# Second MLP product with 512-column matmuls over all eight PSUM banks, and a third late buffer for weights

## The chip, the cores and the metric

The kernel runs on one core of one Trainium2 chip. Its time is the device time of one launch in microseconds (us); less is better. The core has five engines that run side by side and each take their instructions strictly in the order written: TensorE (PE, matrix products), VectorE (DVE), ScalarE (ACT), GpSimd (POOL) and SyncE (SP, which here only issues transfers). Transfers from memory, whoever issues them, are carried by 16 DMA engines that all queues share. Matrix products write to PSUM, a small memory of eight banks, each with 512 single-precision columns on 128 partitions.

## The reference

One decoder layer over 512 tokens with 1024 features. Only its end matters here, the squared-ReLU MLP and the final norm:

```python
def rms_norm(x, g):
    xf = x.astype(jnp.float32)
    y = xf * lax.rsqrt(jnp.mean(xf * xf, axis=-1, keepdims=True) + NORM_EPS)
    return (y * g.astype(jnp.float32)).astype(x.dtype)
...
        x = x + cross_attention(h, mem_n, w_xq[l], w_xk[l], w_xv[l], w_xo[l])
        h = rms_norm(x, norm_mlp[l])
        x = x + jnp.square(jax.nn.relu(h @ w_ff1[l])) @ w_ff2[l]
    return rms_norm(x, norm_final)
```

`w_ff1` is 1024 x 4096 and `w_ff2` is 4096 x 1024. Before the MLP come a combined projection, two kinds of mixing heads, an output projection and a cross-attention; the change does not touch them.

## The kernel before

**Split operands.** Every large product works on numbers split in two: `hi`, rounded by ACT to the matrix unit's reduced format, and `lo`, the rest, which DVE subtracts. A product then takes three matmuls for each pair of 128 x 128 weights and its activations: upper weights with upper activations, upper weights with lower activations, lower weights with upper activations. Weights arrive in units of 128 x 1024, that is eight blocks. The function `split_raw` turns a unit that has landed in a raw buffer into `wh` (ACT, 1024 columns) and `wl` (DVE, 1024 columns).

**The two MLP products.** Each is a 2 x 2 block product done in the seven-product way (Strassen in Winograd's form), so it needs sums of weight blocks and sums of activation blocks. Tokens are cut into two halves of 256, so a matmul there has 256 columns.

The *first* product runs `f1_group(j)` for j = 0 to 7. A group has seven steps, one for each product, of 2 x 4 x 3 = 24 matmuls. Its weights come as transfers named A, B, C, c and D (`f1_load`, L277). B and c get a second block added on the way by a GpSimd transfer; D and the later meaning of A are made by DVE sums (`f1_add`). `f1_prep(j, s)` (L288) is called two steps ahead of the matmuls that use its unit (`SPLIT_AHEAD`); it emits the split of one unit and, at fixed s, the loads of the group after: B at s = 1, C at 3, A at 4, c at 5, D at 6. B, C and c rotate over three raw buffers (`RAWS`), A and D over two buffers of the late pool (`raw_tile`, L227). The results of the steps are taken out of PSUM by `evac` inside `f1_group`, on ACT and DVE; some of that work is put off into a list, `rest`, which the next step runs.

The *second* product (`PLAN`, L1287, and the loop below it) runs seven products p of eight weight units each: units 0 to 3 are the first half of the contraction for the four output tiles n, units 4 to 7 the second half. A unit has 8 x 3 = 24 matmuls of 256 columns, a product 192, the whole 1344. The accumulators X, Y and Z are pairs of banks; a bank holds two output tiles of 256 columns. X is used by products 0, 2, 4 and 6, which go on adding to what it holds, Y by 1 and 3, Z by 5. After each pair of output tiles DVE adds the bank (128 x 2 x 256) into the residual `x1`; from product 3 on, ACT and DVE also do their share of the final norm (`norm_part`). For each product ACT and DVE also split four activation tiles (`make_op`, tiles `op`, 128 x 2048: upper half and lower half side by side), and DVE makes the sums of activation blocks (`make_sum`, tiles `g`), four each for products 2, 3 and 4.

**What sets the order.** From `f1_group` on, the order on each engine is the order in which the program emits instructions (`manual_schedule`). In the second product a unit begins with `need`, which emits the loads as far ahead as buffers allow (at most `RAWS + 2` = 5 raw units open) and the split of the unit two ahead; then `f1_rest`, `need_op` and `need_sum`, then the matmuls, then the evacuation. `wl` rotates over three buffers, so the DVE split of the unit two ahead waits until PE has finished the unit before.

In PSUM eight banks are two pools of four, `pacc` (X, Z) and `pside` (Y and small things). In SBUF the late pool lies where the early pool (`ep`) was. Some weight sums for the second product (tiles `u`) are made in DRAM by transfers of SP and of POOL during the first product (`more_sums`).

Nearly all instructions pass through the helper at L115, so the profile shows that line for them; they are told apart by the names of their tiles.

Of the kernel before, what the change touches and what calls it, by code (L numbers as in the profile page):

```python
# [8 lines left out]
F32 = mybir.dt.float32  # L9
# [6 lines left out]
P = 128  # L16
D = 1024
T = 512
M = 256
# [12 lines left out]
MLP = 8 + 8 + 4 + 8 + 4 + 4 + 4 + 4 + 8 + 8 + 8  # L32
FF2 = MLP + 7 * 8
# [89 lines left out]
def hybrid_layer(ctx: ExitStack, tc: tile.TileContext, xT, memT, ws, vecs, consts, rots, out):  # L123
    nc = tc.nc
    pace = Pace()
    V, A, PE = (pace.engine(e, t) for e, t in ((nc.vector, "dve"), (nc.scalar, "act"), (nc.tensor, "pe")))
    SY, PO = pace.engine(nc.sync, "dma"), pace.engine(nc.gpsimd, "pool")
    cpool = ctx.enter_context(tc.tile_pool(name="cpool", bufs=1))
# [2 lines left out]
    dram = ctx.enter_context(tc.tile_pool(name="dram", bufs=1, space=bass.MemoryType.DRAM))  # L131
    early = ExitStack()
    ep = early.enter_context(tc.tile_pool(name="early", bufs=1, reuse_waits="tile"))
    pacc = ctx.enter_context(tc.tile_pool(name="pacc", bufs=4, space=bass.MemoryType.PSUM))
    pside = ctx.enter_context(tc.tile_pool(name="pside", bufs=4, space=bass.MemoryType.PSUM))
    ordered = tc.manual_schedule()
    ordered.__enter__()
    WBUFS, N8, N2, N2E, N8L = 4, 12, 14, 8, 3
# [21 lines left out]
    def acc_bank(name):  # L160
        return pacc.tile([P, T], F32, tag="acc", name=name)

    def side_bank(name):
        return pside.tile([P, T], F32, tag="ps", name=name)
# [5 lines left out]
    raws, his, los, late, n8 = {}, {}, {}, [], [1]  # L170
    state = {"load": 0, "split": 0}
    LOAD_AHEAD, SPLIT_AHEAD, RAWS = 6, 2, 3
# [13 lines left out]
    def two(ap):  # L186
        return ap.rearrange("p (n c) -> p n c", n=2)
# [11 lines left out]
    def add(dst, src):  # L199
        return nc.gpsimd.dma_start(dst, src, accum_op=ALU.add, max_dma_last_dim=4 * D)  # L200
# [25 lines left out]

    def raw_tile(name, in_late):  # L227
        if in_late:
            return late[0].tile([P, D], F32, tag="rawl", name=name, bufs=2)
        return wpool.tile([P, D], F32, tag="raw", name=name, bufs=RAWS)  # L230

    def load_unit(parts=((0, D),)):
        u = state["load"]
        raws[u] = raw_tile(f"wr{u}", u >= FF2 and (u - FF2) % 5 in (1, 3))
        for a, b in parts:
            SY.dma_start(raws[u][:, a:b], sources[u][:, a:b])
        state["load"] += 1
        if SUMS_FROM <= u < MLP:
            more_sums()
# [37 lines left out]
    def f1_load(j, what):  # L277

        r, c = {"A": (0, 0), "B": (0, 0), "C": (1, 1), "D": (1, 0)}[what.upper()]
        t = f1raw[what, j] = raw_tile(f"w{what}{j}", what in "AD")  # L280
        nc.sync.dma_start(two(t), E[r][c][j].rearrange("n p c -> p n c"))
        if what in "Bc":
            nc.gpsimd.dma_start(two(t), E[0][1][j].rearrange("n p c -> p n c"), accum_op=ALU.add)
# [4 lines left out]
    def f1_prep(j, s):  # L288

        split_raw(split_begin(), f1raw[("ABCAcDd" if j == 7 else "ABDCAcD")[s], j], 0, D)  # L290
        if s == 1:
            f1_add(j, "A", "B", "C")
        if j == 7:
            if s == 1:
                f1_load(j, "d")
                state["load"] = FF2
            elif s > 2:
                load_unit()
            if s == 3:
                f1_add(j, "d", "d", "A")  # L300
        elif s == 1:
            f1_load(j + 1, "B")
        elif s == 3:
            f1_add(j, "D", "D", "A")
            f1_load(j + 1, "C")
        elif s == 4:
            f1_load(j + 1, "A")
        elif s == 5:
            f1_load(j + 1, "c")
        elif s == 6:  # L310
            f1_load(j + 1, "D")
        if s in (2, 6):
            more_sums()

    def need(u):
        marks.append(last_mm[0])
        if MLP <= u + SPLIT_AHEAD < FF2:
            f1_prep(*divmod(u + SPLIT_AHEAD - MLP, 7))
            return
        last = MLP if u < MLP else UNITS  # L320
        most = RAWS if u < MLP else RAWS + 2
        want_load, want_split = min(last, u + LOAD_AHEAD + 1), min(last, u + SPLIT_AHEAD + 1)
        while state["split"] < want_split or state["load"] < want_load:
            if state["load"] < want_load and state["load"] - state["split"] < most:
                load_unit()
            elif state["split"] < want_split:
                split_unit()
            else:
                break
        if MLP - 6 <= u < MLP - 2:  # L330
            for what in ("A", "B", "CD", "c")[u - MLP + 6]:
                f1_load(0, what)
# [53 lines left out]
    def mm(o, l, r, start, stop):  # L386
        last_mm[0] = PE.matmul(o, l, r, start=start, stop=stop, skip_group_check=True)
        since[0] += 1
        if since[0] >= GAP:
            pump()  # L390
# [223 lines left out]
    u = 4  # L614
# [242 lines left out]
        yield from norm_rows(S, M, rbm, rcm)  # L857

    mem = {}
    rbm = cpool.tile([P, M], F32, name="rbm")  # L860
    rcm = cpool.tile([P, 2], F32, name="rcm")
    fm_stage(u, x_act, T, ev_g, "hg", ONE * 4)
    u += 4
# [325 lines left out]
    def need_sum(i):  # L1189
        while sum_state[0] < min(28, i + 1):  # L1190
            make_sum(*divmod(sum_state[0], 4))
            sum_state[0] += 1
# [3 lines left out]
    def make_op():  # L1196

        i = op_state[0]
        op_state[0] += 1
        need_sum(i)  # L1200
        src = OPS[i // 4](i % 4)
        both = l8(F32R, f"op{i}").rearrange("p a b -> p (a b)")
        hi, lo = (x.rearrange("p (k c) -> p k c", k=4) for x in (both[:, :D], both[:, D:]))
        if i // 4 == 2:
            A.activation(hi, src, AF.Copy, scale=-1.0)
            V.scalar_tensor_tensor(lo, src, -1.0, hi.bitcast(F32), op0=ALU.mult, op1=ALU.subtract)
        else:
            A.activation(hi, src, AF.Copy)
            V.tensor_sub(lo, src, hi.bitcast(F32))
        ops[i] = [(hi[:, k], lo[:, k]) for k in range(4)]  # L1210

    def need_op(i):
        while op_state[0] < min(28, i + 1):
# [5 lines left out]
        f1_group(j)  # L1219
        u += 7  # L1220

    X, Z = ([acc_bank(f"{x}{b}") for b in range(2)] for x in "XZ")
    Y = [side_bank(f"Y{b}") for b in range(2)]

    def place(h, t, b):

        return x1[h][:, 2 * b:2 * b + 2, t * half:(t + 1) * half]

    def into(h, t, op):
        def evac(banks, n):  # L1230
            if n % 2:
                d = place(h, t, n // 2)
                getattr(V, op)(d, d, two(banks[n // 2]))
        return evac

    rbf = rb2
# [19 lines left out]

    def final_half(nb, S, q):

        ps = side_bank("fs")
        yield [S[:, :half]]  # L1260
        smm(ps[:, :half], ones, S[:, :half], True, False)
        yield [q[:, :half]]
        smm(ps[:, :half], ones, q[:, :half], False, True)
        r = rbf[:, nb * half:(nb + 1) * half]
        rsqrt_of(r, ps[:, :half], D)
        for eng, a, b in ((V, 0, 2), (V, 2, 4), (V, 4, 7), (V, 7, 8)):
            x = xg(nb, a, b)
            eng.tensor_mul(x, x, r[:, None, :].to_broadcast([P, b - a, half]))
            SY.dma_start(out[nb, :, a:b], x)

    def ends(h, t, op):
        add = into(h, t, op)

        def evac(banks, n):
            add(banks, n)
            if n % 2:
                norm_part(h, t, n - 1)
                norm_part(h, t, n)
        return evac

    def ends_last(banks, n):
        d = x1[0][:, n, half:]
        V.tensor_add(d, d, two(banks[n // 2])[:, n % 2])
        norm_part(0, 1, n)


    PLAN = ((X, True, into(0, 0, "tensor_add")), (Y, True, into(1, 1, "tensor_sub")),  # L1287
            (X, False, into(1, 0, "tensor_sub")), (Y, False, ends(1, 0, "tensor_sub")),
            (X, False, ends(1, 1, "tensor_sub")), (Z, True, ends(0, 0, "tensor_add")), (X, False, ends_last))

    for p, (banks, begins, after) in enumerate(PLAN):
        for j in range(8):
            i, c, n = 8 * p + j, j // 4, j % 4
            if i >= 52:
                n = LAST[n]
            need(FF2 + i)
            f1_rest()
            need_op(4 * p + 2 * c + 1 + (0, 1, 2, 2)[j % 4])
            need_sum(4 * p + 2 * c + (3, 3, 3, 4)[j % 4])
            hi, lo = his[FF2 + i], los[FF2 + i]  # L1300
            acc = two(banks[n // 2])[:, n % 2]
            for k in range(8):
                a_hi, a_lo = ops[4 * p + 2 * c + k // 4][k % 4]
                w_hi, w_lo = hi[:, k * P:(k + 1) * P], lo[:, k * P:(k + 1) * P]
                mm(acc, w_hi, a_hi, begins and c == 0 and k == 0 and n % 2 == 0, False)
                mm(acc, w_hi, a_lo, False, False)
                mm(acc, w_lo, a_hi, False, c == 1 and k == 7)
            if c:
                after(banks, n)
    drain(("fin", 0))  # L1310
    drain(("fin", 1))
    ordered.__exit__(None, None, None)
# [74 lines left out]
```

## Time and profile before

| | |
|---|---|
| runs | 758.73, 760.60, 762.17 us; median 760.60 us |
| profiled execution | 756.95 us, of it 755.2 us span (first to last instruction) |
| PE busy | 735.1 us, 97% of the span, 4696 matmuls |
| DVE busy | 545.5 us, 72% |
| ACT busy | 415.5 us, 55% |
| mean granted TensorE clock | 0.996 of full speed |
| first MLP product | matmuls start from 413.06 us to 582.79 us |
| second MLP product | from 582.91 us; the last matmul is over at 746.03 us |
| after it | final norm of the last half and stores, to 755.2 us |

A group of the profile names the tile written, the tiles read, the shape, how many instructions and their mean duration. The durations of matmuls overlap, since they are pipelined: a matmul of 256 columns is shown as 283 ns long, while the next one starts 120 ns after it. What a matmul costs in a full stretch is therefore read from the distance between starts, or from a row of the chain of waits, which gives a stretch's length and the number of matmuls in it. The chain of waits follows the execution back from its last instruction to whatever released each step.

### The profile page before, as it was taken

What the parts mean: (1) busy time and instruction counts of PE and PEld (TensorE: products, weight loads), DVE (VectorE), ACT (ScalarE), POOL (GpSimd) and SP (SyncE); (2) the same over time, 40 slices, a digit from 0 to 9 for tenths busy, and PEclk for the clock granted to TensorE, in tenths of its full rate; (3) what the DMA queues carried; (4) which work ended last, traced back from release to release, by engine and by line L of the source; (5) the groups of instructions that cost most, each with busy time, mean ns of one, the idle gap of its engine ahead of it and who ended that gap; (6) DMA issues with size and microseconds to landing.
All of it is one profiled execution on the core that took longest, in us unless ns stands there. A gap on an engine that the chain in (4) does not pass through costs nothing.

```text
span 755.2 us, 11996 instructions
## 1 busy us (share of the span) xinstructions
PE 735.1 (97%) x4696; PEld 664.0 (88%) x4696; DVE 545.5 (72%) x891; ACT 415.5 (55%) x634; POOL 49.4 (7%) x62
## 2 busy tenths in 40 slices
PE   7999999999999999999999999998999999999995
PEld 5888888777787998888888999998899999999995
DVE  6898554887766656767377878786778778877783
ACT  6773447345855454545365655465446655546562
POOL 1000000000111200011000111221110000000000
PEclk9999999999999999999999999999999999999999
DMA  7425334544689996479726688898975655545641
GB/s 274 149 76 167 112 116 135 167 135 132 183 207 238 207 313 258 118 160 278 254 77 147 169 249 221 187 208 215 212 213 169 204 189 193 173 162 168 207 156 57
DMA packets 44441, 137.03 MB, mean 181 GB/s; under 512 B 4544, under 2 KB 6976, under 8 KB 43744
## 3 DMA queue, kind: packets, MB, share of 16 engines
q1 hardware_dynamic: 34944, 110.64, 42.8%
q0 software_dynamic: 8960, 25.17, 19.1%
q8 instruction: 37, 0.61, 0.3%
q10 hardware_dynamic: 480, 0.45, 0.2%
q14 instruction: 20, 0.16, 0.1%
HBM read 134.15 MB, written 35.65 MB: 225 GB/s over the span
## 4 chain that ended last, share of the span: by engine, by line
PE 87%; DMA 4%; ACT 3%; DVE 3%; issue 2%; SPq 0%; DVEq 0%; ACTq 0%
PE X L115 19%; PE Y L115 12%; PE xo L115 7%; PE mkq L115 6%; PE xq L115 6%; PE wo L115 5%; DMA wA<-in_ws_dram 3%; PE hf L115 3%; PE Z L115 3%; PE hg L115 3%; PE mv L115 3%; PE memv L115 3%; PE hq L115 3%; PE hi L115 3%; PE memk L115 2%
## 5 line engine op out<-in xcount | busy, mean ns | idle before, releaser
L115 ACT ACTIVATE wh<-wr 128x1024 fp32r<-128x1024 f32 (+2 forms) x126 | 130.4, 1041 | 121.2 <-PE wo L115 19.6
L115 DVE TENSOR_TENSOR wl<-wr,wh 128x1024 fp32r<-128x1024 f32 (+2 forms) x126 | 151.5, 1205 | 40.7 <-ACT wh L115 26.4
L115 PE MATMUL X<-op,wh 128*128 128x256 f32 x512 | 92.7, 283 | 0.0
L115 PEld LDWEIGHTS X<-op,wh 128*128 128x128 f32 x512 | 79.9, 192 | 0.1
L115 PE MATMUL X<-op,wl 128*128 128x256 f32 x256 | 72.7, 284 | 0.6 <-DVE wl L115 0.6
L200 POOL DMA_DIRECT2D u<-in_ws_dram x32 | 31.0, 968 | 328.5 <-PE hg L115 201.1
L115 PEld LDWEIGHTS X<-op,wl 128*128 128x128 f32 x256 | 49.1, 192 | 0.8 <-DVE wl L115 0.8
L115 PE MATMUL Y<-OS,wh 128*128 128x256 f32 x256 | 47.2, 284 | 0.2 <-ACT t L115 0.2
L115 PE MATMUL X<-OS,wh 128*128 128x256 f32 x256 | 46.5, 283 | 0.0
L115 PE MATMUL Y<-op,wh 128*128 128x256 f32 x256 | 46.2, 283 | 0.0
L115 PEld LDWEIGHTS Y<-OS,wh 128*128 128x128 f32 x256 | 39.9, 192 | 0.5 <-ACT t L115 0.4
L115 PEld LDWEIGHTS Y<-op,wh 128*128 128x128 f32 x256 | 39.9, 192 | 0.0
L115 PEld LDWEIGHTS X<-OS,wh 128*128 128x128 f32 x256 | 39.9, 192 | 0.0
L115 PE MATMUL Y<-op,wl 128*128 128x256 f32 x128 | 36.2, 283 | 0.0
L115 PE MATMUL X<-OS,wl 128*128 128x256 f32 x128 | 36.2, 283 | 0.0
L115 PE MATMUL Y<-OS,wl 128*128 128x256 f32 x128 | 36.2, 283 | 0.0
L115 ACT ACTIVATE g<-t 128x512 f32<-128x512 f32 x32 | 19.0, 624 | 29.2 <-DVE t L115 29.2
L115 ACT ACTIVATE op<-g 128x1024 fp32r<-128x1024 f32 x28 | 29.2, 1045 | 0.5 <-PE X L115 0.5
L115 DVE TENSOR_TENSOR op<-g,op 128x1024 fp32r<-128x1024 f32 x24 | 29.3, 1219 | 0.0
L115 ACT ACT_TABLE_LOAD x22 | 28.2, 1283 | 1.5 <-PEq L1375 1.2
L115 PE MATMUL mkq<-xhi,wh 128*128 128x512 f32 x64 | 26.7, 417 | 0.0
L115 ACT ACTIVATE t<-X 128x256 f32<-128x256 f32 x32 | 11.3, 375 | 27.8 <-PE X L115 27.7
(312 smaller groups left out, 2114.2 us busy)
## 6 DMA issues: line engine op xcount, KB each, us to landing
wr<-in_ws_dram SPq DMA_DIRECT2D x90, 512.0 KB, 4.3
u<-in_ws_dram POOLq DMA_DIRECT2D x32, 512.0 KB, 7.7
wr<-u SPq DMA_DIRECT2D x32, 512.0 KB, 3.4
u<-in_ws_dram SPq DMA_DIRECT2D x16, 512.0 KB, 3.9
u<-u SPq DMA_DIRECT2D x16, 512.0 KB, 4.7
wA<-in_ws_dram SPq DMA_DIRECT2D x8, 512.0 KB, 6.5
wD<-in_ws_dram SPq DMA_DIRECT2D x8, 512.0 KB, 6.3
wB<-in_ws_dram SPq DMA_DIRECT2D x8, 512.0 KB, 4.3
```

Of the source, the lines that this page charges most:

```text
L115: return f(*args, **kw)
L200: return nc.gpsimd.dma_start(dst, src, accum_op=ALU.add, max_dma_last_dim=4 * D)
```

## The change

- In the second product, the matmul of upper weights with upper activations and that of upper weights with lower activations become one: the moving operand is the pair of 256-column pieces (upper, lower), the result 512 columns, a whole bank. The matmul of lower weights with upper activations adds into that bank's first half. Each output tile now has its own bank, so each accumulator has four banks; X and Y take all eight, and Z's product uses Y again. The two first PSUM pools are closed for this and one of its own is opened.
- Taking a result out means adding both halves of a bank, so `into` and `ends_last` do two DVE additions where there was one. For products 0 to 5 they are put off to the next unit by way of `rest`.
- Sums of activation blocks are emitted two operands earlier (`need_sum`).
- The late pool's raw tag gets three buffers instead of two; in the first product the load of A moves from s = 4 to s = 2; in the second, raw tiles alternate between the pools and up to six may be open instead of five. The tile `rbm` moves to the early pool.

```diff
-    pacc = ctx.enter_context(tc.tile_pool(name="pacc", bufs=4, space=bass.MemoryType.PSUM))
-    pside = ctx.enter_context(tc.tile_pool(name="pside", bufs=4, space=bass.MemoryType.PSUM))
+    banks1 = ExitStack()
+    pacc, pside = (banks1.enter_context(tc.tile_pool(name=n, bufs=4, space=bass.MemoryType.PSUM)) for n in ("pacc", "pside"))
...
-            return late[0].tile([P, D], F32, tag="rawl", name=name, bufs=2)
+            return late[0].tile([P, D], F32, tag="rawl", name=name, bufs=RAWS)
...
-        raws[u] = raw_tile(f"wr{u}", u >= FF2 and (u - FF2) % 5 in (1, 3))
+        raws[u] = raw_tile(f"wr{u}", u >= FF2 and (u - FF2) % 2 == 1)
...
+        elif s == 2:
+            f1_load(j + 1, "A")
         elif s == 3:
             f1_add(j, "D", "D", "A")
             f1_load(j + 1, "C")
-        elif s == 4:
-            f1_load(j + 1, "A")
...
-        most = RAWS if u < MLP else RAWS + 2
+        most = RAWS if u < MLP else 2 * RAWS
...
-        ops[i] = [(hi[:, k], lo[:, k]) for k in range(4)]
+        ops[i] = [both.rearrange("p (x k c) -> p x k c", x=2, k=4)[:, :, k] for k in range(4)]
...
+    banks1.close()
+    pm = ctx.enter_context(tc.tile_pool(name="pm", bufs=1, space=bass.MemoryType.PSUM, reuse_waits="tile"))
+
+    def banks4(name):
+        return [pm.tile([P, 2, T], F32, tag=f"{name}{b}", name=f"{name}{b}", bufs=1) for b in range(2)]
 
     def into(h, t, op):
-        def evac(banks, n):
+        def evac(acc, n):
             if n % 2:
-                d = place(h, t, n // 2)
-                getattr(V, op)(d, d, two(banks[n // 2]))
+                d = x1[h][:, n - 1:n + 1, t * half:(t + 1) * half]
+                for x in range(2):
+                    getattr(V, op)(d, d, acc[n // 2][:, :, x * half:(x + 1) * half])
         return evac
...
-    def ends_last(banks, n):
+    def ends_last(acc, n):
         d = x1[0][:, n, half:]
-        V.tensor_add(d, d, two(banks[n // 2])[:, n % 2])
+        for x in range(2):
+            V.tensor_add(d, d, acc[n // 2][:, n % 2, x * half:(x + 1) * half])
         norm_part(0, 1, n)
...
+    accs = {name: banks4(name) for name in "YX"}
+    for p, (name, begins, after) in enumerate(PLAN):
+        if p == 5:
+            accs[name] = banks4(name)
+        acc = accs[name]
...
-            need_sum(4 * p + 2 * c + (3, 3, 3, 4)[j % 4])
+            need_sum(4 * p + 2 * c + (5, 5, 5, 6)[j % 4])
             hi, lo = his[FF2 + i], los[FF2 + i]
-            acc = two(banks[n // 2])[:, n % 2]
             for k in range(8):
-                a_hi, a_lo = ops[4 * p + 2 * c + k // 4][k % 4]
+                a = ops[4 * p + 2 * c + k // 4][k % 4]
                 w_hi, w_lo = hi[:, k * P:(k + 1) * P], lo[:, k * P:(k + 1) * P]
-                mm(acc, w_hi, a_hi, begins and c == 0 and k == 0 and n % 2 == 0, False)
-                mm(acc, w_hi, a_lo, False, False)
-                mm(acc, w_lo, a_hi, False, c == 1 and k == 7)
-            if c:
-                after(banks, n)
+                mm(two(acc[n // 2][:, n % 2]), w_hi, a, begins and c == 0 and k == 0, False)
+                mm(acc[n // 2][:, n % 2, :half], w_lo, a[:, 0], False, c == 1 and k == 7)
+            if c and p < 6:
+                rest.append(lambda after=after, acc=acc, n=n: after(acc, n))
+            elif c:
+                after(acc, n)
```

What moves on PE, at the start of the second product (X is the accumulator, `op` the split activations, `wh` and `wl` the two parts of the unit's weights). Before:

```order
L115 MATMUL X_5808<-op_5634,wh_5738 128x256 x2
L115 MATMUL X_5808<-op_5634,wl_5739 128x256
L115 MATMUL X_5808<-op_5634,wh_5738 128x256 x2
L115 MATMUL X_5808<-op_5634,wl_5739 128x256
L115 MATMUL X_5808<-op_5634,wh_5738 128x256 x2
L115 MATMUL X_5808<-op_5634,wl_5739 128x256
```

After:

```order
L115 MATMUL X_5817<-op_5634,wh_5738 128x512
L115 MATMUL X_5817<-op_5634,wl_5739 128x256
L115 MATMUL X_5817<-op_5634,wh_5738 128x512
L115 MATMUL X_5817<-op_5634,wl_5739 128x256
L115 MATMUL X_5817<-op_5634,wh_5738 128x512
L115 MATMUL X_5817<-op_5634,wl_5739 128x256
```

Three matmuls of 256 columns have become one of 512 and one of 256; the number of columns is the same, the number of matmuls falls from 1344 to 896.

What moves on SP, in the first product, at the loads for groups 5 and 6 (the names are the transfers A to D). Before:

```order
L281 DMA wB_4796<-in_ws_dram 128x2x512
L281 DMA wC_4872<-in_ws_dram 128x2x512
L281 DMA wA_4908<-in_ws_dram 128x2x512
L281 DMA wc_4945<-in_ws_dram 128x2x512
L281 DMA wD_4976<-in_ws_dram 128x2x512
L281 DMA wB_5042<-in_ws_dram 128x2x512
```

After:

```order
L281 DMA wB_4796<-in_ws_dram 128x2x512
L281 DMA wA_4835<-in_ws_dram 128x2x512
L281 DMA wC_4874<-in_ws_dram 128x2x512
L281 DMA wc_4945<-in_ws_dram 128x2x512
L281 DMA wD_4976<-in_ws_dram 128x2x512
L281 DMA wB_5042<-in_ws_dram 128x2x512
```

The load of A now stands right behind that of B, ahead of C, and before c and D as before.

What moves on DVE, in product 2 of the second MLP product, around the first half of the results (x is the residual, X the accumulator). Before:

```order
L115 TENSOR_TENSOR wl_6492<-wr_6361,wh_6491 128x1024
L115 TENSOR_TENSOR op_6495<-g_3834,op_6495 128x1024
L115 TENSOR_TENSOR x_1899<-x_1899,X_5808 128x2x256
L115 TENSOR_TENSOR wl_6526<-wr_6394,wh_6525 128x1024
L115 TENSOR_TENSOR op_6529<-g_3835,op_6529 128x1024
```

After:

```order
L115 TENSOR_TENSOR wl_6333<-wr_6234,wh_6332 128x1024
L115 TENSOR_TENSOR op_6336<-g_3834,op_6336 128x1024
L115 TENSOR_TENSOR wl_6358<-wr_6259,wh_6357 128x1024
L115 TENSOR_TENSOR x_1899<-x_1899,X_5817 128x2x256 x2
L115 TENSOR_TENSOR op_6363<-g_3835,op_6363 128x1024
```

The addition out of PSUM has become two, and they stand behind the next weight split instead of ahead of it.

More of the change, by code (lines that the diff above doesn't have):

```diff
@@ L859, in hybrid_layer @@
     mem = {}
-    rbm = cpool.tile([P, M], F32, name="rbm")
+    rbm = ep.tile([P, M], F32, name="rbm")
     rcm = cpool.tile([P, 2], F32, name="rcm")
@@ L1220, in hybrid_layer @@
         u += 7
[L1222 to L1227, printed above, removed]
+    banks1.close()
+    pm = ctx.enter_context(tc.tile_pool(name="pm", bufs=1, space=bass.MemoryType.PSUM, reuse_waits="tile"))
+    def banks4(name):
+        return [pm.tile([P, 2, T], F32, tag=f"{name}{b}", name=f"{name}{b}", bufs=1) for b in range(2)]
     def into(h, t, op):
-        def evac(banks, n):
+        def evac(acc, n):
             if n % 2:
-                d = place(h, t, n // 2)
-                getattr(V, op)(d, d, two(banks[n // 2]))
+                d = x1[h][:, n - 1:n + 1, t * half:(t + 1) * half]
+                for x in range(2):
+                    getattr(V, op)(d, d, acc[n // 2][:, :, x * half:(x + 1) * half])
         return evac
@@ L1257, in final_half @@
     def final_half(nb, S, q):
-        ps = side_bank("fs")
+        ps = banks4("Y")[0][:, 0]
         yield [S[:, :half]]
@@ L1272, in ends, with evac @@
         add = into(h, t, op)
-        def evac(banks, n):
-            add(banks, n)
+        def evac(acc, n):
+            add(acc, n)
             if n % 2:
@@ L1279, in ends @@
         return evac
-    def ends_last(banks, n):
+    def ends_last(acc, n):
         d = x1[0][:, n, half:]
-        V.tensor_add(d, d, two(banks[n // 2])[:, n % 2])
+        for x in range(2):
+            V.tensor_add(d, d, acc[n // 2][:, n % 2, x * half:(x + 1) * half])
         norm_part(0, 1, n)
[L1287 to L1291, printed above, removed]
+    PLAN = (("X", True, into(0, 0, "tensor_add")), ("Y", True, into(1, 1, "tensor_sub")),
+            ("X", False, into(1, 0, "tensor_sub")), ("Y", False, ends(1, 0, "tensor_sub")),
+            ("X", False, ends(1, 1, "tensor_sub")), ("Y", True, ends(0, 0, "tensor_add")), ("X", False, ends_last))
+    accs = {name: banks4(name) for name in "YX"}
[3 more added lines that the diff above has]
+        acc = accs[name]
         for j in range(8):
```

## The prediction

> **What bounds the kernel now.** I read the page first: the span, then the busy shares.
>
> ```profile
> span 755.2 us, 11996 instructions
> PE 735.1 (97%) x4696; PEld 664.0 (88%) x4696; DVE 545.5 (72%) x891; ACT 415.5 (55%) x634; POOL 49.4 (7%) x62
> ```
>
> PE is busy almost throughout, so time goes down in two ways only: the same products in fewer PE nanoseconds, or fewer holes. For the price of a matmul I read the chain of waits in order of time, where a row is a stretch, its length in us and its number of matmuls. Stages of 512 columns, then one product of the second MLP product:
>
> ```profile
> 128.37 10.47 PE mkq L115 x46
> 182.20 3.24 PE hg L115 x14
> 278.15 15.88 PE xq L115 x70
> 364.59 48.63 PE xo L115 x214
> ...
> 629.16 23.04 PE X L115 x192
> ```
>
> The last row gives 23.04 / 192 = 0.1200 us for each matmul of 256 columns. Those of 512 cost 48.63 / 214 = 0.2272 (xo), 15.88 / 70 = 0.2269 (xq), 0.2276 (mkq), 0.2314 (hg). So 256 more columns cost 0.1072 us, and a matmul of 256 costs 0.0128 us beyond its columns: a price for each matmul, whatever its length. The three matmuls of a weight block pay it three times.
>
> For the holes I read the waits of PE from 400 to 585 us (total, times, longest), then the chain there:
>
> ```profile
> PE X L115 <- DVE t L115: 4.7, 3, 2.7
> PE Y L115 <- ACT t L115: 0.2, 1, 0.2
> ```
>
> ```profile
> 484.00 7.33 DMA wA<-in_ws_dram
> ...
> 505.24 9.27 DMA wA<-in_ws_dram
> ...
> 528.40 8.34 DMA wA<-in_ws_dram
> ```
>
> PE is named as waiting for a DVE evacuation (t), but the chain leads back to the load of A, three groups running. ACT, DVE and PE of the second case, in order of time:
>
> ```profile
> 514.58 1.06 ACT L115 ACTIVATE wh<-wA 128x1024 fp32r<-128x1024 f32 x1 [3.95 <-DMA wA<-in_ws_dram]
> 515.55 1.04 ACT L115 ACTIVATE wh<-wB 128x1024 fp32r<-128x1024 f32 x1
> ```
>
> ```profile
> 515.67 1.23 DVE L115 TENSOR_TENSOR wl<-wA,wh 128x1024 fp32r<-128x1024 f32 x1 [3.56 <-ACT wh L115]
> 516.82 0.41 DVE L115 TENSOR_TENSOR t<-t,X 128x256 f32<-128x256 f32 x1
> ```
>
> ```profile
> 514.25 0.28 PE L115 MATMUL X<-OBh,wl 128*128 128x256 f32 x1
> 517.28 0.39 PE L115 MATMUL X<-OBh,wh 128*128 128x256 f32 x1 [2.75 <-DVE t L115]
> ```
>
> ACT stood 3.95 us until A landed; DVE stood behind ACT; the evacuation of X, which needs nothing of A, stood behind that split in DVE's queue; and PE could not reuse X.
>
> **The change part by part.**
>
> *A's load (third buffer, s = 4 to s = 2).* SP's issues for one group:
>
> ```profile
> 496.40 0.37 SPq L281 DMA_DIRECT2D wB<-in_ws_dram  x1
> 502.97 0.37 SPq L281 DMA_DIRECT2D wC<-in_ws_dram  x1
> 505.24 0.37 SPq L281 DMA_DIRECT2D wA<-in_ws_dram  x1
> ```
>
> With two buffers A had to wait until the old A was split. With three it takes the buffer of a D that was used up a group earlier, stands right behind B in SP's queue, and can go at about 496.8 instead of 505.24: 8.4 us earlier, against ACT's wait of 3.95. What the holes cost: the two rows above are 3.03 us apart, where 0.12 is normal, so 2.91. The others:
>
> ```profile
> 493.66 0.28 PE L115 MATMUL X<-OBh,wl 128*128 128x256 f32 x1
> 494.11 0.39 PE L115 MATMUL X<-OBh,wh 128*128 128x256 f32 x1 [0.17 <-DVE t L115]
> ...
> 537.42 0.28 PE L115 MATMUL X<-OBh,wl 128*128 128x256 f32 x1
> 539.52 0.39 PE L115 MATMUL X<-OBh,wh 128*128 128x256 f32 x1 [1.82 <-DVE t L115]
> ...
> 543.63 0.41 PE L115 MATMUL X<-OA,wh 128*128 128x256 f32 x2
> ```
>
> They give 0.45 - 0.12 = 0.33 and 2.10 - 0.12 = 1.98. From 539.52 to 543.63 there are 21 matmuls in 4.11 us, where 21 x 0.12 = 2.52 were due: 1.59 more. The clock granted shows why:
>
> ```profile
> 540.00:550.00 10.00, 10.00 (x74) 10.00 (x73) 8.41 (x11) 6.52 (x12) 1.26 (x2) 0.83 0.80 168
> ```
>
> Clock 0.83 (the third number from the end) over ten us is half clock for 3.4 us; so the hole brought a slow stretch with it, which goes too. Sum 2.91 + 0.33 + 1.98 + 1.59 = **6.8 us**. The Trainium skill (TensorE: Matmul & The Clock Gate, HAM oscillation) has the clock fall only after idle gaps of more than about 3.4 us, while here 1.82 us did it and 2.75 us did not; by the rule alone the slow stretch would have another cause and could stay, and the term would be 5.2.
>
> What may be late next is B, whose second block POOL adds:
>
> ```profile
> 501.51 1.23 POOL L283 DMA_DIRECT2D wB<-in_ws_dram  x1 [3.59 <-DMA wB<-in_ws_dram]
> ```
>
> and among the DMA issues the time from issue to landing, 7.0 us in the median:
>
> ```profile
> wB<-in_ws_dram POOLq DMA_DIRECT2D x8, 512.0 KB, 7.0
> ```
>
> So it lands near 501.51 + 7.0 = 508.5. Without the wait for A, ACT comes to B at 514.58 - 3.95 + 1.0 = 511.6. Three us of slack, about what one more 512 KB transfer ahead of it takes. C, c and D are issued as before and no longer share the engines with A. Bounds: 6.8 at most; 3.4, half, if B inherits the wait. I take 6.8, since the lead is twice the wait.
>
> *The matmuls.* 7 products x 8 units x 8 blocks = 448 triples. Before 3 x 0.1200 = 0.3600 us; now 0.2272 + 0.1200 = 0.3472; 448 x 0.0128 = **5.7 us**. No row shows a matmul whose moving operand is two pieces 4 KB apart, as it is now. Ends: no price for it at all, 0.2144 (11.5 us gained); the whole price for each piece, 0.2400 (nothing gained); and twice that, 0.2528 (5.7 us lost). I take the 512-column rows, since the columns and results are the same and only the addresses jump. With hg's 0.2314 it would be 3.8.
>
> *DVE.* 12 more additions of 128 x 2 x 256 in products 0 to 5, and 4 of 128 x 256 in the last: 12 x 0.69 + 4 x 0.42 = 10 us of DVE. Its fullest product (the fourth number is DVE's busy time):
>
> ```profile
> 629.00:652.00 23.00, 23.00 (x194) 23.00 (x193) 20.04 (x18) 12.29 (x12) 0.00 (x0) 1.00 0.53 183
> ```
>
> and the group of its additions out of X, 686 ns each:
>
> ```profile
> L115 DVE TENSOR_TENSOR x<-x,X 128x512 f32<-128x512 f32 x6 | 4.1, 686 | 3.4 <-PE X L115 3.4
> ```
>
> 20.04 + 2 x 0.69 = 21.4 us in a product that will take 64 x 0.3472 = 22.2. It fits, with little left; moving the sums two operands ahead shifts part of this into product 0. I take 0. Behind a put-off addition stand the splits of operands and weights, due one to two units (2.8 to 5.6 us) later. An accumulator bank is needed again only two products later (one, for what Y's next product takes over), so the delay itself is hidden.
>
> *The end.* After the last matmul the chain is serial, so the second addition is paid in full:
>
> ```profile
> 746.05 0.43 DVE x L115
> 746.49 0.02 issue
> 746.51 0.42 ACT fsq L115
> ```
>
> Plus **0.45 us**.
>
> *Start of the second product.* X now lies on banks that Y's pool held, so its first matmul waits for the last Y addition:
>
> ```profile
> 581.98 0.41 DVE L115 TENSOR_TENSOR t<-t,Y 128x256 f32<-128x256 f32 x1
> ...
> 582.91 0.40 PE L115 MATMUL X<-op,wh 128*128 128x256 f32 x2
> ```
>
> Over at 582.39, needed at 582.91: hidden by 0.5 us; were DVE 1 us later, 0.5 us lost. I take 0. The sixth raw buffer and `rbm` I take at 0 as well: PE waits 0.6 us at most for splits in the second product, and `rbm` is read only long before.
>
> Sum: -6.8 - 5.7 + 0.45 = **-12.0 us**. The profiled execution, 756.95 us (its span 755.2), becomes 744.9. It lay below all three runs shown; their median is 760.6, so on their scale the forecast is **748.6**.
>
> **The rivals.**
>
> *The jump costs a start.* If the second piece pays the 0.0128 again, only A's term is left: 760.6 - 6.8 + 0.45 = 754.3. For it: no row shows such an operand. Against: 256 matmuls in a row pay the price with a weight load each, and the fused one has a single load. The Trainium skill (TensorE: Matmul & The Clock Gate, Back-to-back issue gap) gives a fixed 2.5 ns per matmul; with it, as an estimate, 1.1 us would be gained instead of 5.7, which is 753.2, in this case's place; the trace has 12.8 ns.
>
> *The wait moves.* Transfers are 87% of what 16 engines can do from 470 to 540 us:
>
> ```profile
> 470.00:540.00 70.00, 65.25 (x540) 64.64 (x539) 50.40 (x69) 36.31 (x54) 13.66 (x14) 1.00 0.87 215
> ```
>
> If B's addition, or c, now lands late by what A did, only the matmuls gain: 760.6 - 5.7 + 0.45 = 755.4; half, 752.0. Against: the order of loads is spread better, and each other load has more lead than A had.
>
> *Slower: DVE sets the pace in products 0 to 3.* If DVE's work in a product passes 22.2 us by more than the lead of its splits (about 4 us), PE waits for `wl`, and a hole of about 2 us can bring 1.6 us of half clock. Once in each of four products that is 4 x (2.3 + 1.6) = 15.6: 760.6 - 12.0 + 15.6 = 764.2. It needs some 5 us more DVE work per product than the rows give; little speaks for it.
>
> *Better still.* If the 3.65 us by which the median exceeds the profiled execution are longer waits for A, they go too: 744.9. That the change doesn't do what it says I exclude: the order shows 512-column matmuls and A behind B.
>
> **How the numbers follow.** Forecast (747 to 751 with the scatter of the runs): 0.58. Better still: 0.12. Jump: 0.12. Wait moves: 0.13. DVE, slower: 0.05. The predicted time is the likeliest's, 748.6. The range goes from 744 (better still) to 756 (both single-gain cases); it leaves out the slower case and the tails. Half a per cent, 3.8 us, is about what a measurement of this kernel can tell from no change; 756.8 is the border. Faster: 0.58 + 0.12 + most of 0.25 = 0.88. Within: 0.08, the cases of single gain at their bad ends. Slower: 0.04.
>
> **What would show it.** Right: stretches of the second product in which a 512 and a 256 together take 0.347 us, a product of 22.2 us; no wait of PE for t behind A, clock 1.00 from 400 to 585 us; DVE above 90% in products 1 to 3 without PE waiting for it; a second addition of 0.4 us in the final chain. Wrong: 0.36 per pair (jump); ACT waiting for wB or wc by DMA, with PE holes at 490 to 540 (wait moves); PE waiting for `wl` or `op` in products 0 to 3 (DVE).

## The result, and the profile after

The changed kernel takes **746.98 us** in the median (746.78 to 747.39, 6 runs) where the kernel before, run beside it, took 758.68 us (757.20 to 762.17, 6 runs): a ratio of 0.9841, 95% interval 0.9818 to 0.9863. The profiled execution took 747.39 us, with a span of 745.6 us, against 756.95 and 755.2 before. Profile against profile the gain is 9.6 us, median against median 11.7 us; the forecast had 12.0 and 748.6 us. So the time came out as forecast, but one of its two large terms did not, and the experiments below are mostly about why.

The page after, span, busy times and the chain by engine (before, PE held 87% of the chain, with 4% for DMA and 3% each for ACT and DVE):

```profile
span 745.6 us, 11110 instructions
...
PE 728.1 (98%) x4248; PEld 636.2 (85%) x4248; DVE 553.9 (74%) x907; ACT 415.4 (56%) x634; POOL 49.5 (7%) x62
...
PE 94%; DVE 2%; DMA 1%; ACT 1%; issue 1%; DVEq 0%; ACTq 0%
```

The chain of waits after, in order of time (start, length, engine, tile, matmuls), from the middle of the first MLP product into the second:

```profile
507.15 11.52 PE X L115 x96
518.67 8.64 PE Y L115 x72
...
573.44 25.49 PE X L115 x152
598.93 22.62 PE Y L115 x128
```

No load of A stands in it any more: a group of the first product is 168 matmuls in 20.16 us, exactly 0.1200 each. The waits of PE over both products (total, times, longest), all that there are from 400 to 745 us:

```profile
PE Y L115 <- ACT fsq L115: 1.0, 1, 1.0
PE X L115 <- DVE x L115: 0.3, 1, 0.3
PE Y L115 <- ACT t L115: 0.2, 1, 0.2
```

The 4.7 us for t behind A are gone, and so is the slow stretch of the clock (the third number from the end; 0.83 before in the same ten us):

```profile
540.00:550.00 10.00, 10.00 (x86) 10.00 (x85) 8.83 (x11) 5.17 (x8) 1.25 (x1) 1.00 1.06 231
```

SP's issues of one group, A now right behind B, 9 us earlier than before:

```profile
495.57 0.37 SPq L281 DMA_DIRECT2D wB<-in_ws_dram  x1
496.03 0.42 SPq L281 DMA_DIRECT2D wA<-in_ws_dram  x1
```

The waits of ACT in the first product, from 410 to 585 us, show where the wait went. After the change, and then before it:

```profile
ACT wh L115 <- DMA wc<-in_ws_dram: 4.2, 3, 2.4
```

```profile
ACT wh L115 <- DMA wA<-in_ws_dram: 8.5, 4, 3.9
```

Half of it moved to another transfer, c, but PE pays for none of that: the longest such wait, 2.4 us, stays inside the lead that the splits have. B, too, now comes a little late once, by 0.30 us; ACT at that moment:

```profile
511.70 1.06 ACT L115 ACTIVATE wh<-wB 128x1024 fp32r<-128x1024 f32 x1 [0.30 <-DMA wB<-in_ws_dram]
```

In the second product a product is 22.61 us, where 23.04 stood before and 22.2 was forecast. DVE's busy time is the fourth number of the second row, a window of 23 us; over exactly one product (598.93 to 621.55 us) DVE is busy 21.1 us of 22.6, or 93%:

```profile
621.55 22.61 PE X L115 x128
```

```profile
622.00:645.00 23.00, 23.00 (x132) 19.94 (x131) 21.47 (x21) 12.68 (x13) 0.00 (x0) 1.00 0.56 185
```

The end of the chain, with the second addition:

```profile
734.94 1.05 PE X L115 x6
...
736.01 0.43 DVE x L115
...
736.47 0.43 DVE x L115
...
736.92 0.42 ACT fsq L115
```

The 9.6 us between the profiles add up from four stretches. Their borders are read from the chain, in both kernels alike: a row of X holds the last 24 matmuls of the first product, 0.12 us each, and the first product of the second. After, that is the row at 573.44 above, so the border lies at 573.44 + 2.88 = 576.32 us; before, it is this row, and the border lies at 580.20 + 2.88 = 583.08:

```profile
580.20 25.92 PE X L115 x216
```

Up to the first product: 413.68 us before, 413.92 after, +0.24. (The first matmul of X before starts at 413.51 us by its own row; the 413.06 in the table of the kernel before is a matmul of xo.) First product: 169.40 us (413.68 to 583.08) against 162.40 (413.92 to 576.32), **-7.00**. Second product up to its last matmul: 162.95 against 159.67 us, **-3.28**. From there to the end: 9.17 against 9.61, +0.44.

### The profile page after: what moved, and what is told of

Same layout as the page of the kernel before. It is cut to its first block, busy times and chain, and to the rows that moved or that the text cites. A ratio compares the mean times of both kernels' runs of the same rounds, so it can differ in the third digit from the quotient of the medians.

```text
span 745.6 us, 11110 instructions
## 1 busy us (share of the span) xinstructions
PE 728.1 (98%) x4248; PEld 636.2 (85%) x4248; DVE 553.9 (74%) x907; ACT 415.4 (56%) x634; POOL 49.5 (7%) x62
## 4 chain that ended last, share of the span: by engine, by line
PE 94%; DVE 2%; DMA 1%; ACT 1%; issue 1%; DVEq 0%; ACTq 0%
PE X L115 23%; PE Y L115 19%; PE xo L115 7%; PE mkq L115 6%; PE xq L115 6%; PE wo L115 5%; PE hg L115 3%; PE mv L115 3%; PE memv L115 3%; PE hq L115 3%; PE hi L115 3%; PE memk L115 2%; PE hf L115 2%; PE xs L115 2%; PE a L115 1%; PE sc L115 1%
## 5 line engine op out<-in xcount | busy, mean ns | idle before, releaser
L115 PE MATMUL X<-op,wh 128*128 128x512 f32 x256 | 90.6, 398 | 0.3 <-DVE x L115 0.3
L115 PE MATMUL Y<-op,wh 128*128 128x512 f32 x192 | 68.0, 399 | 0.0
L115 PEld LDWEIGHTS X<-op,wh 128*128 128x128 f32 x256 | 48.1, 188 | 12.1 <-issue 0.5
L115 PE MATMUL Y<-op,wl 128*128 128x256 f32 x192 | 53.9, 281 | 0.0
L115 PEld LDWEIGHTS Y<-op,wh 128*128 128x128 f32 x192 | 36.1, 188 | 9.0
L115 PEld LDWEIGHTS Y<-op,wl 128*128 128x128 f32 x192 | 36.3, 189 | 0.0
```

The costliest lines, as they stand in the source:

```text
L115: return f(*args, **kw)
```

## The experiments

All of them were timed beside runs of the kernel before on the same chip. The median of before in these groups of runs lay between 757.9 and 758.8 us.

### A's load alone

What the second product's change is worth, and whether A's load explains the rest. The kernel before, with the third late buffer and A at s = 2 (`rbm` goes to the early pool for room):

```diff
-            return late[0].tile([P, D], F32, tag="rawl", name=name, bufs=2)
+            return late[0].tile([P, D], F32, tag="rawl", name=name, bufs=RAWS)
...
+        elif s == 2:
+            f1_load(j + 1, "A")
...
-        elif s == 4:
-            f1_load(j + 1, "A")
```

> The kernel before with only the load of A moved to s = 2, the third late buffer and rbm in the early pool; the second product as before. Theory: the holes of PE behind A are gone, clock 1.00 through the first product, first product 162.4 us as in the changed kernel, profiled time 756.95 - 6.8 = 750.1; the runs also stop scattering by 5 us if that scatter was the waits for A, and the median falls by 6.8 to 9 against the kernel before. Rival (the gain of the first product comes from elsewhere in the change): less than 3 us.

Measured: 750.39 us (749.86 to 750.59), ratio 0.9882 (0.9855 to 0.9909). Its chain is as regular as that of the changed kernel in the first product, which takes the same 162.4 us, with the old price in the second:

```profile
507.56 11.52 PE X L115 x96
519.08 8.64 PE Y L115 x72
...
622.81 23.04 PE X L115 x192
```

So the load is worth 8.4 us in the median, and what is left to the second product is 750.39 - 746.98 = 3.4 us. It also takes the scatter away: the runs of this kernel lie within 0.7 us, those of before, run beside it, within 5.8 (755.65 to 761.45). So most of the scatter of before lies in its waits for A, and the profiled execution of before, 756.95 us, was probably one with short waits: its own holes gave 6.8, the medians 1.6 more. This is inferred from the times; no longer execution of before was profiled.

### The place without the buffer, the buffer without the place

The changed kernel with A's load back at s = 4, three buffers kept:

```diff
-        elif s == 2:
-            f1_load(j + 1, "A")
...
+        elif s == 4:
+            f1_load(j + 1, "A")
```

> The changed kernel with the load of A back at s = 4, the third buffer kept. Theory (place in SP's queue decides, the buffer alone is not enough): A can go only behind C, about 2 us earlier than before the change, against a wait of 3.95; most of the holes are back, 3 to 7 us slower than the changed kernel, 750 to 754, and the scatter of the runs is back. Rival (the third buffer alone frees A): as the changed kernel, 747, no holes.

Measured: 752.78 us (751.81 to 753.64). The changed kernel with two late buffers, A's load at s = 2:

```diff
-            return late[0].tile([P, D], F32, tag="rawl", name=name, bufs=RAWS)
+            return late[0].tile([P, D], F32, tag="rawl", name=name, bufs=2)
...
-        raws[u] = raw_tile(f"wr{u}", u >= FF2 and (u - FF2) % 2 == 1)
+        raws[u] = raw_tile(f"wr{u}", u >= FF2 and (u - FF2) % 5 in (1, 3))
...
-        most = RAWS if u < MLP else 2 * RAWS
+        most = RAWS if u < MLP else RAWS + 2
```

> The changed kernel with the load of A at s = 2 but with two late buffers, as before the change. Theory (place and buffer are one term: with two buffers the load at s = 2 must wait on SP until the old A is split at s = 4, and C is queued behind it): the holes of the first product are back and the time is 753 to 756 us, no better than with the place undone (752.8). Rival (the place alone is what counts): 747 us like the changed kernel.

Measured: 755.15 us (753.23 to 755.99). SP's issues in this kernel show why the place alone is worth next to nothing:

```profile
497.37 0.37 SPq L281 DMA_DIRECT2D wB<-in_ws_dram  x1
506.21 0.37 SPq L281 DMA_DIRECT2D wA<-in_ws_dram  x1
506.63 0.90 SPq L281 DMA_DIRECT2D wC<-in_ws_dram  x1
```

A stands second in the queue but goes 8.8 us after B, since SP waits for the buffer, and C now waits behind it. The holes of PE between 400 and 585 us, first with the buffer alone, then with the place alone:

```profile
PE X L115 <- DVE t L115: 3.8, 2, 3.5
PE Y L115 <- ACT t L115: 0.6, 2, 0.4
```

```profile
PE X L115 <- DVE t L115: 5.0, 3, 3.0
PE Y L115 <- ACT t L115: 2.5, 2, 2.3
```

Neither half of this edit does what both do: 5.8 us are lost with one, 8.2 with the other. The second of these kernels also lacks the sixth raw buffer, and its second product takes 159.7 us as in the changed kernel, so that buffer is worth nothing there.

### Why a pair costs 0.3533 us

A block is one matmul of 512 columns and one of 256. 22.61 us / 64 = 0.3533 us, 6.1 ns more than 0.2272 + 0.1200. The first suspicion was the operand, two pieces 4 KB apart. Here they are laid side by side, so that the operand is 512 columns in a row:

```diff
-        hi, lo = (x.rearrange("p (k c) -> p k c", k=4) for x in (both[:, :D], both[:, D:]))
+        pairs = both.rearrange("p (k x c) -> p k x c", k=4, x=2)
+        hi, lo = pairs[:, :, 0], pairs[:, :, 1]
...
-        ops[i] = [both.rearrange("p (x k c) -> p x k c", x=2, k=4)[:, :, k] for k in range(4)]
+        ops[i] = [pairs[:, k] for k in range(4)]
```

> The changed kernel with each operand's upper and lower pieces laid side by side, so that the 512-column matmul reads 512 columns in a row instead of two pieces 4 KB apart; nothing else differs. In the changed kernel a 512 and a 256 together take 22.61 / 64 = 0.3533 us, where 0.3472 was forecast. Theory jump (the second piece costs part of a start): a pair takes 0.3467 to 0.3475 us, a product 22.2 us, the kernel is 448 x 0.0065 = 2.9 us faster than the changed one, about 744. Theory mix (a 512 next to a 256 costs more than in a stretch of its own kind): 0.3533 us, 22.6 us a product, about 747, no change.

Measured: 747.12 us (746.76 to 747.26), and the same product to the last digit:

```profile
621.14 22.61 PE X L115 x128
```

The jump costs nothing. Next, the alternation of sizes: in each unit eight matmuls of 512 and then eight of 256.

```diff
...
-                mm(two(acc[n // 2][:, n % 2]), w_hi, a, begins and c == 0 and k == 0, False)
-                mm(acc[n // 2][:, n % 2, :half], w_lo, a[:, 0], False, c == 1 and k == 7)
+                mm(two(acc[n // 2][:, n % 2]), hi[:, k * P:(k + 1) * P], a, begins and c == 0 and k == 0, False)
+            for k in range(8):
+                a = ops[4 * p + 2 * c + k // 4][k % 4]
+                mm(acc[n // 2][:, n % 2, :half], lo[:, k * P:(k + 1) * P], a[:, 0], False, c == 1 and k == 7)
```

> The changed kernel with the eight 512-column matmuls of a unit first and its eight 256-column ones after them, operands as in the changed kernel (pieces 4 KB apart). Theory jump: the 512s still take 0.2333 us each, a unit 2.827 us, the time stays at 747 (within 0.5). Theory mix: 0.2272 and 0.1200 in their own stretches, a unit 2.78 us, about 2.7 us less, 744.

Measured: 746.19 us (746.02 to 746.39). Products of the chain:

```profile
620.92 22.35 PE X L115 x128
643.27 22.35 PE Y L115 x128
665.61 22.57 PE X L115 x128
```

Part of the price went, not all of it. (Products 4 and 5 hold one stretch each in which two matmuls of 512 stand 0.11 us longer than usual; why is open.) One more kernel gives each product its own order of the same blocks; in product 1 the lower weights meet both halves too, so that all its matmuls are 512 wide:

```diff
+                if p == 1:
+                    mm(two(bank), lo[:, k * P:(k + 1) * P], a, False, c == 1 and k == 7)
...
+                size = (1, 1, 1, 8, 4, 2, 1)[p]
+                for b in range(0, 8, size):
+                    turn = (lower, upper) if p == 3 and j % 2 else (upper, lower)
+                    for f in turn:
+                        for k in range(b, b + size):
+                            f(k)
```

> One kernel, a different order of the same weight blocks in each product of the second MLP product. Product 1: both matmuls of a block 512 columns wide (the lower weights meet both halves too, which adds the lower-times-lower term). Product 2: three matmuls of 256 as before the change. Product 3: eight of 512 then eight of 256 in even units, the other way round in odd ones. Product 4: four and four. Product 5: two and two. Theory switch (a 512 costs 0.2267 us once the matmuls before it were 512 wide too, and some 6 to 9 ns more only in the first five after a change from 256): product 1 takes 128 x 0.2267 = 29.0 us, product 2 23.04, product 3 about 22.3, products 4 and 5 about 22.45 (beside any wait). Theory operand (a 512 whose operand is both halves costs 0.2333 wherever it stands): product 1 takes 128 x 0.2333 = 29.9 us, products 3, 4 and 5 take 22.6 like the changed kernel.

Measured, in the one execution timed, 753.43 us, of which the rows of the chain for products 1 to 5 are what counts:

```profile
598.75 29.08 PE Y L115 x128
627.82 23.03 PE X L115 x192
650.86 22.29 PE Y L115 x128
673.15 22.43 PE X L115 x128
695.58 22.31 PE Y L115 x128
```

Product 1: 29.08 / 128 = 0.2272 us, with the same operand of both halves. So a 512 of that kind has the price of any other, once its neighbours are 512 wide too. With eight and eight, half of them in turned order, the pair is 22.29 / 64 = 0.3483. The distances between the starts of matmuls in the trace, here of product 3 in ns, show the price as a disturbance behind each change from 256 to 512:

```
256s: 120 120 120 120   512s: 233 236 228 233 231 226 227 227 226 227 227 226 227 ...   256s: 113 119 120 120
```

Five matmuls are late, by 6, 9, 1, 6 and 4 ns, and the first 256 after the change back is 7 ns early: 19 ns for a change. In the strict alternation of the changed kernel no 512 ever gets past it: there the distances go round in three pairs, 233 + 117, 241 + 120 and 236 + 113, together 1060 ns, which is 3 x 353.3. Two and two came out at 22.31, below the 22.45 expected, so the lateness is not just the sum of these five; what sets it inside TensorE stays open.

### How much room DVE has

The prediction set DVE's ten us more at nothing. Here two further additions stand at every put-off evacuation of products 0 to 5 (the second addition is taken back and done again):

```diff
-                for x in range(2):
-                    getattr(V, op)(d, d, acc[n // 2][:, :, x * half:(x + 1) * half])
+                back = "tensor_sub" if op == "tensor_add" else "tensor_add"
+                for x, o in ((0, op), (1, op), (1, back), (1, op)):
+                    getattr(V, o)(d, d, acc[n // 2][:, :, x * half:(x + 1) * half])
```

> The changed kernel with two more additions out of PSUM at each put-off evacuation of products 0 to 5 (the second one taken back and done again: 2 x 2 x 0.69 = 2.76 us more DVE per product, about 24.2 us of DVE in a product of 22.6 us where the changed kernel has 21.5). Theory (DVE is hidden with little left, and only the lead of its splits stands between it and PE): products 1 to 3 fall behind by up to 1.6 us each, the first of it covered by a lead of about 4 us, so 0.5 to 5 us are lost: 747.5 to 752 us, with PE waiting for wl or op in product 2 or 3. Rival (DVE is far from setting the pace): 747 us, no wait. Rival (DVE already sets it at the margin): 16 us more, 763 us.

Measured: 758.30 us (757.46 to 758.56): 11.3 us lost, the whole gain of the change. That is more than the 0.5 to 5 us expected and less than the 16 of the second rival; PE waits for `op` and `wl` from product 2 on, 8.3 us in all. The same with the two extra additions at only one of a product's two evacuations (n == 1):

> The changed kernel with the two further additions at one of the two put-off evacuations of products 0 to 5 only: 1.38 us more DVE per product, 22.9 us in products 1 and 2, where PE needs 22.6. Twice as much cost 11.3 us. Theory (a threshold: nothing is lost while what DVE falls behind, about 0.3 us in each of products 1 to 3, is less than the lead of its splits): 747 to 748 us. Rival (no threshold, PE pays for each us of DVE): half of 11.3 us, 752.6 us.

Measured: 750.88 us (750.70 to 751.22): 3.9 us lost, where the theory expected 1 us at most and the rival half of 11.3. The waits of PE in the second product of this kernel, and windows of 23 us over about products 1, 2 and 4:

```profile
PE X L115 <- DVE op L115: 1.7, 2, 0.8
...
PE Y L115 <- DVE op L115: 0.8, 1, 0.8
```

```profile
599.00:622.00 23.00, 23.00 (x132) 19.96 (x131) 22.59 (x24) 12.67 (x13) 0.00 (x0) 1.00 0.56 184
622.00:645.00 23.00, 23.00 (x133) 19.95 (x132) 22.58 (x23) 12.67 (x14) 0.00 (x0) 1.00 0.53 183
...
668.00:691.00 23.00, 22.39 (x126) 19.36 (x127) 18.54 (x21) 13.78 (x21) 0.00 (x0) 1.00 0.54 183
```

In products 1 and 2 DVE is full (22.6 of 23 us) and PE never waits. PE waits afterwards, once each early in products 4, 5 and 6 (at 668.6, 692.4 and 716.1 us), where DVE has time to spare (4.5 us in the third row). What happens there shows on ACT, in order of time, at the end of product 3 in this kernel:

```profile
657.79 1.06 ACT L115 ACTIVATE wh<-wr 128x1024 fp32r<-128x1024 f32 x1 [0.81 <-PE Y L115]
664.82 0.42 ACT L115 ACTIVATE Sf<-x 128x256 f32<-128x256 f32 x1 [5.97 <-DVE x L115]
...
665.85 0.49 ACT L115 ACTIVATE g<-x,vec 128x256 f32<-128x256 f32 x1
666.25 1.04 ACT L115 ACTIVATE op<-g 128x1024 fp32r<-128x1024 f32 x1
```

From product 3 on, ACT's squares for the final norm wait for the addition on DVE, and the next splits of operands and weights stand behind them in ACT's queue. In the changed kernel this wait of ACT is 4.52 us and PE pays nothing; with 5.97 it pays. The arrears of DVE are paid at this point, once a product, and DVE's free time later does not make them good, because each split is then a chain: addition, squares, upper half, lower half, matmul.

The change moved two things that bear on this: the additions were put off behind the next unit's splits, and the operand sums were made two operands earlier. Both undone:

```diff
-            need_sum(4 * p + 2 * c + (5, 5, 5, 6)[j % 4])
+            need_sum(4 * p + 2 * c + (3, 3, 3, 4)[j % 4])
...
-            if c and p < 6:
-                rest.append(lambda after=after, acc=acc, n=n: after(acc, n))
-            elif c:
+            if c:
                 after(acc, n)
```

> The changed kernel with the additions out of PSUM and the operand sums where they stood before the change (the additions at once instead of behind the next unit's splits, the sums two operands later); DVE does the same work in another order. Theory (a pair of additions is now 1.4 us of DVE and stands ahead of the next split; the lead of the splits is one to two units, 2.8 to 5.6 us, and covers it): 747 us, no wait of PE for wl in products 1 to 3. Rival (the margin of DVE is thin, as the run with more additions showed, and the order decides whether it is enough): waits of PE for wl or op in products 1 to 5, 749 to 753 us.

Measured: 750.69 us (750.39 to 752.56): 3.7 us more than the changed kernel, so the rival was right. Then one by one. Only the additions at once again:

> The changed kernel with the additions out of PSUM at once again, and the sums two operands early as in the changed kernel. Both undone cost 3.7 us. Theory (what costs is the chain addition on DVE, squares on ACT that wait for it, next weight split on ACT behind them, its lower half on DVE, PE; it is the place of the additions that sets it): 749.5 to 751 us, with PE waiting for wh or wl from product 3 on. Rival (it is the lead of the operand sums): 747 us.

Measured: 749.66 us (749.30 to 750.37), 2.7 us lost. Only the sums late again:

> The changed kernel with the operand sums where they stood before the change and the additions put off as in the changed kernel. Theory: 747 us, or 748 at most. Rival (it is the lead of the sums that gives DVE its margin in products 1 to 3): 749.5 to 751 us, with PE waiting for op.

Measured: 747.87 us (747.49 to 748.27), 0.9 us lost. The waits of PE in the second product, with the additions at once:

```profile
PE X L115 <- DVE wl L115: 1.5, 2, 0.8
...
PE Y L115 <- DVE wl L115: 0.8, 1, 0.8
```

2.7 and 0.9 add up to 3.6, about the 3.7 of both. Without these two edits the longer matmuls would have earned nothing: 750.69 us against the 750.39 of A's load alone.

### A version that beats both

Three edits to the changed kernel: grouped sizes, in odd units the other way round; the last unit's upper half added in ahead of its second pass, which then runs on 256 columns; the final norm's multiplications of the first half spread over the last product.

```diff
...
+            for f in (lower, upper) if j % 2 and p < 6 and not (begins and c == 0) else (upper, lower):
+                for k in range(8):
+                    f(k)
+            if i == 51:
+                rest.append(lambda acc=acc: V.tensor_add(x1[0][:, 3, half:], x1[0][:, 3, half:], acc[1][:, 1, half:]))
...
+            yield 2.0
             x = xg(nb, a, b)
```

> The changed kernel with three edits: (1) in each unit of the second MLP product eight matmuls of 512 and then eight of 256, in odd units of products 0 to 5 the other way round where the bank is not begun, so fewer changes of size; (2) the last unit's upper half of results is added in ahead of its second pass, which then runs with three matmuls of 256, so one addition of 0.43 us leaves the final chain; (3) the four multiplications of the final norm of the first half are spread over the last product instead of standing together ahead of weight splits on DVE. Theory: (1) 0.8 us as measured by grouping alone plus some 0.3, (2) 0.4, (3) about 0.5 to 1 of the 1.4 us that the last product takes beyond the others: 746.98 - 2.2 = 744.8 us. If (1) is bound to the place of the splits on DVE and not to the size change, odd units wait for wl and the time is 746 to 749.

Measured: **744.70 us** (744.44 to 744.95), ratio to before 0.9815 (0.9795 to 0.9835). Its chain, products 2 and 5 and the first and last stretch of product 6:

```profile
620.46 22.27 PE X L115 x128
...
687.26 22.31 PE Y L115 x128
709.56 5.32 PE X L115 x30
...
730.42 3.13 PE X L115 x24
```

Products 0 to 5 together are 1.9 us shorter than in the changed kernel, the end 0.46 (742.7 - 733.55 = 9.15 us after the last matmul, against 9.61). The three edits were not run one by one. The third did nothing that shows: the last product takes 23.99 us in both (709.56 to 733.55 here, 712.00 to 735.99 in the changed kernel). In the changed kernel that is 1.4 us more than the products ahead of it, and its chain shows where most of this lies, in the norm's own matmuls on PE, which no order on DVE takes away:

```profile
717.53 0.54 PE Y L115 x2
...
718.77 0.43 PE Y L115 x2
```

These are 1.0 us; the other 0.4 is the gap ahead of one matmul at 732.96 us, which waited for an addition (x).

## Why the prediction was right, point by point

**A's load: the mechanism was right, and so, nearly, was the size in the profile.** Forecast -6.8 from the profiled holes, measured -7.0 between the profiles. That the half clock of 1.59 us belonged to the hole was right too: with the hole it went (clock 1.00). The term of 5.2, which the Trainium skill's rule on idle gaps (TensorE: Matmul & The Clock Gate, HAM oscillation) would have given, does not agree with these rows. But the term was sized on one execution. The median execution of before has 1.6 us more of such waits (8.4 by A's load alone). By the medians, then, part of the rival "better still" held; the 3.65 us that it took came from three runs only, and over the six runs given above the median of before lies 1.7 us above the profiled execution.

**The matmuls: right mechanism, wrong size.** The step that failed is "448 x (0.3600 - 0.3472) = 5.7 us". The rows used for 0.2272 and 0.1200 are stretches of one size; the changed kernel alternates sizes, and there the pair costs 0.3533, so the price saved is 6.7 ns for a block and not 12.8: 448 x 0.0067 = **3.0 us** of the 3.3 measured. The other 0.3 is not taken apart here; one wait of PE for `wl`, 0.6 us before and gone after, is of that size. The row of hg (0.2314 a matmul, forecast 3.8) pointed that way and was named but not taken, though no run shows that its price has the same cause. The rival "jump" is refuted: adjacent pieces cost the same. By the Trainium skill's issue gap of 2.5 ns a matmul (TensorE: Matmul & The Clock Gate, Back-to-back issue gap) 1.1 us were to be gained, an estimate too low for these rows.

**The wait moves: half true, at no price.** ACT now waits 4.2 us for c, and for B once 0.3 us, where three us of slack were forecast. PE pays for neither.

**DVE at nothing: right, for a reason that was too comfortable.** The forecast was 21.4 us in the fullest product, and the trace has 21.1. Of the sign "above 90% in products 1 to 3" only products 1 and 2 hold (93%); product 3 has 84%. "It needs some 5 us more DVE work per product than the rows give" was wrong: 1.4 us more per product cost 3.9 us, 2.8 cost 11.3. The lead of the splits was counted as a cushion for each product, and it was not seen that ACT's norm work ties DVE's additions to the next split from product 3 on. The sentence that the new order of additions and sums is hidden was also incomplete: this order is what keeps DVE at nothing, worth 3.7 us.

**The end and the start of the second product: right.** +0.45 forecast, +0.44 measured; no wait at the first matmul of X; the sixth raw buffer at nothing, as the kernel with the place alone shows.

**The sum** is -6.8 - 5.7 + 0.45 = -12.0 in the forecast and -7.0 - 3.3 + 0.44 + 0.24 = -9.6 between the profiles. On the medians it is -11.7. That this is near 12.0 is luck, two errors that cancel: some 2.5 us too much for the second product, some 1.6 too little for A on the scale of the medians. The 748.6 us has a second piece of luck in it. The forecast for a profiled execution was 744.9, and 747.39 came, 2.5 us more; the 3.65 us put on top for the scale of the runs were not there at all, since the median after lies 0.4 us below the profiled execution.

## What to carry to other kernels

Here a load that ended the chain needed its place in the queue and its buffer together: check which tile the issuing queue will wait for once the issue is moved. Price a matmul from a stretch with the same mix of sizes as the planned one, or group equal sizes. And when an engine is called hidden, follow each of its results to the next queue that waits for it: DVE at 93% of a product without a wait was free here, and 1.4 us more was not.

## What the runs showed of the hardware that was not expected

- A matmul of 512 columns costs 0.2267 to 0.2272 us among its like, with an operand in one piece or two, but a pair of a 512 and a 256 in alternation costs 6 ns more than the two prices add up to (353.3 against 347.2 ns); after a run of 256s five matmuls of 512 are late, by 26 ns in all.
- A stretch of half clock behind a hole of PE does not go by the length of the hole here. In the kernel before, 1.82 us of idle time were followed by 3.4 us of half clock and 2.75 us were not (the rows are in the prediction). With the buffer alone, 3.54 us were followed by one (granted clock 0.93 and 0.90 in the ten us before and after 520), and so were 1.19 and 0.76 us close together with the additions and sums as before (0.83 from 670 to 680 us); with the place alone, holes of 3.0 and 2.3 us were not (clock 1.00 throughout). Without the gaps the clock was 1.00 over the whole first product. What decides it stays open.
